# Folding a gate into the output projection's weights and moving the modulation's vectors beside the merge

## The chip, the cores and the metric

The kernel runs on one core of one Trainium2 chip. The metric is the device time in microseconds (us) of one execution; less is better. Matrix products run on TensorE (PE), elementwise work on VectorE (DVE), ScalarE (ACT) and GpSimd (POOL). All transfers of this kernel are issued from the queue of SyncE (SP).

## What is computed

One layer of a streaming encoder: 1024 positions, width 1024, all in float32. Cut to what matters here:

```python
mod = (c_act @ w_ada[l] + b_ada[l])[:, None, :]
shift_t, scale_t, gate_t, shift_f, scale_f, gate_f = jnp.split(mod, 6, axis=-1)

h = x * (1.0 + scale_t) + shift_t
proj = h @ w_in[l]
...
o_a = gated_deltanet(...)          # branch A, 8 heads
o_b = chunk_band_attention(...)    # branch B, 16 heads
gate_a, gate_b = jnp.split(jax.nn.sigmoid(gates + b_gate[l]), N_BRANCHES, axis=-1)
merged = gate_a * (o_a @ w_branch_a[l]) + gate_b * (o_b @ w_branch_b[l])
mix = merged @ w_o[l]
x = layernorm(DEEPNORM_ALPHA * x + gate_t * mix, ln1_g[l], ln1_b[l])

h = x * (1.0 + scale_f) + shift_f
u = causal_dwconv(h @ w_up[l], conv_ffn[l]) + b_conv_ffn[l]
...
x = layernorm(DEEPNORM_ALPHA * x + gate_f * ffn, ln2_g[l], ln2_b[l])
```

`mod` has six vectors of 1024. The first two are needed at the very start. The last four, gate_t, shift_f, scale_f and gate_f, are needed from the output projection on; their weights are 1024 x 4096 values (16 MB).

## The kernel before

The stages follow one another: the input h; branch A's eight heads (some 60 to 860 us of the span); branch B's attention, 16 heads (to about 1343); the merge (to 1456); the output projection with the first layer norm (to 1550); the up projection; the down projection and the last norm. Products are made in three passes: each float32 operand is split into a high and a low part (`split`: a cast, on ACT unless another engine is named, then a subtraction), and high x high, high x low and low x high are summed. A block of weights (128 columns) is loaded into `raw`, a tile with three buffers that are given out in turn, in the order of the program, and split into `wh` and `wl`, also three buffers each (`wblock`, `load_split`). The subtraction of a `wblock` is POOL's.

A planner orders each engine's instructions: among those that its timeline takes for ready, the one that comes first in the program. Each engine, and each DMA queue, then works in the order given.

**The modulation** (`mod_rows`, lines 804 to 827) runs within the loop over branch A's heads, two calls for each head h, 16 in all. A call handles half of the rows of `w_ada` for a block of 512 columns: two loads of 512 KB into `raw`, four DVE instructions that multiply by a column of silu(c) and add into an accumulator (the buffers `gt`, which the merge gates' tiles use too). Behind every second call a product by a matrix of ones sums over the partitions (a full float32 product, two passes on PE), `b_ada` is added to one row, and the row is stored to the DRAM scratch `mod_d`.

**The merge** (lines 1030 to 1067) has 16 blocks: for branch `br` 0 and 1, and j from 0 to 7, a weight block of `w_branch`, 48 products of 128 x 128 by 512, and for each half the gate from scratch (`gates_d`). Branch 0's result stays in the tiles `ma`. Branch 1's is added to it by POOL and split into `mh` and `ml`, which lie where branch A's output was. Behind blocks 5, 6 and 7 of branch 0 the attention's output is loaded and split (`ob`, eight tiles, written to `OB`'s slots); behind branch 1's blocks the eight blocks of `w_o` are loaded and split into `wo`, which take the slots of `ma` and of `ob` as these come free. `OB[i]` and `MA[i]` are lists of slots. Slot B4 holds the attention's group `X` (the buffers `phx`, `plx`), and after it the group `M`, with the ring `macc`.

**The output projection** (`mix`, lines 1102 to 1110) makes 48 products for each of the eight row tiles. Then DVE multiplies the result in PSUM by `gtb` (gate_t / 2, broadcast over the partitions; the half is that of the gates' tanh form), adds ALPHA x, takes statistics, and `norm` applies them on ACT. PE transposes the normed tile, ACT scales and shifts it to the next stage's h (`g1f`, `b1f`), and it is split into `mh` and `ml`. For the scaling, shift_f and scale_f were read back from `mod_d` into rows (`mrow`) and transposed on PE. Of the last row tiles, sums and differences (T2, T3, T4) are built for the up projection, whose products are arranged in a Strassen-like scheme of seven.

Of the kernel before, what the change touches and what calls it, by code (L numbers as in the profile page):

```python
# [73 lines left out]
def _at(group, step_, n, first=0):  # L74
# [30 lines left out]
    "gb": _at("GB", 512, 2), "macc": _at("M", 0, 1),   # L105
    "st": _at("ST", 12, 2), "mv": _at("ST", 4, 4, 36), "gtb": (_E1[0],), "g1b": (_E1[1],),
# [48 lines left out]
def hybrid_layer(  # L155
# [646 lines left out]
    macc = [None]  # L802

    def mod_rows(i):

        cb = i // 2
        if i % 2 == 0:
            macc[0] = ring("gt", [P, 512])
        acc = macc[0]
        for k0 in range(4 * (i % 2), 4 * (i % 2) + 4, 2):  # L810
            rv = W.tile([P, 2, 512], F32, tag="raw", bufs=RB, name=nm("raw"))
            SP.dma_start(rv, w_ada2[k0 * P:(k0 + 2) * P,
                                    2 * D + 512 * cb:2 * D + 512 * cb + 512].rearrange(
                                        "(k p) n -> p k n", p=P))
            for k in (k0, k0 + 1):
                if k == 0:
                    DVE.tensor_scalar(acc, rv[:, 0, :], csil[:, 0:1], None, ALU.mult)
                else:
                    DVE.scalar_tensor_tensor(acc, rv[:, k - k0, :], csil[:, k:k + 1], acc,
                                             ALU.mult, ALU.add)  # L820
        if i % 2 == 1:
            pr_ = mtile(nm("pmod"), "i")
            PE.matmul(pr_, ones, acc, start=True, stop=True)
            row = ring("gt", [P, 512])[0:1, :]
            SP.dma_start(row, b_ada[:, 2 * D + 512 * cb:2 * D + 512 * cb + 512])
            DVE.tensor_tensor(row, row, pr_[0:1, :], ALU.add)
            SP.dma_start(mod_d[:, 512 * cb:512 * cb + 512], row)

# [12 lines left out]
    for h in range(HA):  # L841
        ORD = "sigKq"
        for o in ORD:
            if o == "s":
                with tc.high_priority(offset=PF):
                    stage_solve(h, cs[h])
            elif o == "i":
                with tc.high_priority(offset=PI):
                    stage_inverse(h, cs[h])
            elif o == "K" and h + 1 < HA:  # L850
                with tc.issue_after(last.ins) if last else nullcontext():
                    cs.append(stage_k(h + 1))
            elif o == "g":
                some_gates(GA[h])
            elif o == "q" and h + 1 < HA:
                stage_q(h + 1, cs[h + 1])
        some_gates(GB[h])
        for i in (2 * h, 2 * h + 1):
            mod_rows(i)
        if h + 1 < HA:  # L860
            stage_vz(h + 1, cs[h + 1])
        with tc.high_priority(offset=PC):
            stage_chain(h, cs[h])
        with tc.high_priority(offset=PT):
            stage_out(h, cs[h])
        last = cs[h]["last"]
# [162 lines left out]

    wo = []  # L1030
    for br in range(2):
# [4 lines left out]
        for j in range(NK):  # L1036
            w = wblock(kview(wbr[br], j * P, P), NK)
            for n in range(2):
# [11 lines left out]
                else:  # L1050
# [17 lines left out]


    def bcast(key, src):  # L1070
        t_ = ring(key, [P, D])
        SP.dma_start(t_, src.partition_broadcast(P).rearrange("p o n -> p (o n)"))
        return t_
# [22 lines left out]
    gtb = bcast("gtb", mod_d[:, 0:D])  # L1096
    g1b = bcast("g1b", ln1_g)
    b1b = bcast("b1b", ln1_b)
    DVE.tensor_scalar(gtb, gtb, 0.5, None, ALU.mult)
# [13 lines left out]
    mrow = ring("macc", [P, P])[0:16, :]  # L1113
    SP.dma_start(mrow, mod_d[:, D:3 * D].rearrange("o (r p) -> (o r) p", p=P))
    pmr = pbank("pmr", "t")
    PE.transpose(pmr[:, 0:16], mrow, ident[0:16, 0:16])
    aff = cst.tile([P, 24], F32, tag="aff", name="aff")
    g1f, b1f, s1 = aff[:, 0:8], aff[:, 8:16], aff[:, 16:24]
    g1c, b1c = vt[:, VO["ln1g"]:VO["ln1g"] + 8], vt[:, VO["ln1b"]:VO["ln1b"] + 8]
    DVE.tensor_scalar(s1, pmr[:, 8:16], 1.0, None, ALU.add)  # L1120
    DVE.tensor_tensor(g1f, s1, g1c, ALU.mult)
    DVE.tensor_tensor(b1f, s1, b1c, ALU.mult)
    DVE.tensor_tensor(b1f, pmr[:, 0:8], b1f, ALU.add)
# [3 lines left out]
    for t in range(NT):  # L1127
# [5 lines left out]
        for n in range(2):  # L1133
            N = slice(512 * n, 512 * n + 512)
            DVE.tensor_tensor(m_[:, N], ps[n], gtb[:, N], ALU.mult)
            if t >= MS:
                DVE.scalar_tensor_tensor(r[:, N], r[:, N], ALPHA, m_[:, N], ALU.mult, ALU.add)
        if t < MS:
            DVE.scalar_tensor_tensor(r, r, ALPHA, m_, ALU.mult, ALU.add)
# [26 lines left out]
        if t < NT - 1:  # L1166
            split(mh[:, t], ml[:, t], h32, DVE, DVE)
# [408 lines left out]
```

## Time and profile before

| | |
|---|---|
| median of three runs | 2240.79 us (2235.49 to 2244.45) |
| profiled execution, its own time | 2240.64 us |
| its span, first to last instruction | 2238.9 us |
| mean granted TensorE clock | 0.982 |
| busy share of the span | PE 95%, DVE 71%, ACT 46%, POOL 28% |
| DMA | 220.48 MB, mean 98 GB/s |

The profile is one execution on the chip. Times in it are us from the start of the span. A row of a group gives line, engine, operation, the tile written and those read, shape and count; then busy us, the mean ns of one, and the idle time just before them with what ended most of it. In a timeline, a row is start and duration, and the idle time before it stands in brackets; several instructions of one kind in a row are merged (x2). Rows with SPq are DMA issues. A matmul's duration holds its pipeline, so the distance between two is shorter than one lasts. Line numbers are those of the kernel before.

### The profile page before, as it was taken

Reading aid. Unit: us, or ns where it says so; the run is one execution under the profiler, and the core shown is the slowest. Engines: PE = TensorE matmul, PEld = TensorE weight load, DVE = VectorE, ACT = ScalarE, POOL = GpSimd, SP = SyncE. Lnnn points to the kernel's source line nnn. Section 1 sums busy time; section 2 is a strip of 40 time slices with the busy share of each in tenths; the row PEclk is TensorE's granted clock in tenths of the full one; section 3 lists DMA queues with packets and bytes.
Section 4 is the critical chain, followed back from the end, with each engine's and each line's share of the span. In section 5 each row is a group of like instructions: output and inputs, shape, how many; then the busy total and the mean of one; then the engine's idle time right before and its main releaser. Section 6 shows DMA issues by size and latency. Waiting matters only on the chain.

```text
span 2238.9 us, 31612 instructions
## 1 busy us (share of the span) xinstructions
PE 2129.2 (95%) x11469; PEld 1782.0 (80%) x11469; DVE 1585.5 (71%) x3233; ACT 1025.3 (46%) x2193; POOL 617.0 (28%) x558
## 2 busy tenths in 40 slices
PE   6998999999999999999999999999899999999987
PEld 5687787777878787798989788887688888888875
DVE  8568575765758754567775643458898888889998
ACT  4645243433424334567765642224554444445532
POOL 4323232322323322233432423334110000000064
PEclk9999999999999999999999999999999999999998
DMA  9232333423242412211211523332222222253213
GB/s 284 84 111 73 90 101 105 120 65 117 74 123 80 125 33 98 68 54 47 80 46 59 167 85 128 108 132 94 66 94 85 85 85 85 85 207 110 106 48 131
DMA packets 227263, 220.48 MB, mean 98 GB/s; under 512 B 27354, under 2 KB 184467, under 8 KB 227107
## 3 DMA queue, kind: packets, MB, share of 16 engines
q1 hardware_dynamic: 227027, 218.44, 30.8%
q8 instruction: 90, 1.47, 0.3%
q14 instruction: 66, 0.54, 0.1%
q10 hardware_dynamic: 80, 0.03, 0.0%
HBM read 177.48 MB, written 47.23 MB: 100 GB/s over the span
## 4 chain that ended last, share of the span: by engine, by line
PE 45%; DVE 5%; issue 1%; ACT 1%; POOL 1%; DMA 0%; DVEq 0%; SPq 0%; ACTq 0%; POOLq 0%
PE pup L1282 18%; PE pbr L1043 8%; PE pdn L1460 7%; PE pwo L1107 3%; PE pqk L885 2%; PE pv L900 2%; PE po L975 2%; PE pp L960 1%; PE ps L934 1%; PE pdn L1506 1%; DVE dop L181 0%; DVE hh L1526 0%; DVE hl L181 0%; DMA raw<-in_w_branch_a_dram 0%; DVE G L1163 0%
## 5 line engine op out<-in xcount | busy, mean ns | idle before, releaser
L181 POOL TENSOR_TENSOR wl<-raw,wh 128x1024 fp32r<-128x1024 f32 x88 | 211.4, 2405 | 327.5 <-ACT wh L178 297.9
L1282 PE MATMUL pup<-hh,wop 128*128 128x512 f32 x704 | 229.4, 397 | 5.8 <-ACT SB L1295 3.9
L1282 PE MATMUL pup<-t,wop 128*128 128x512 f32 x792 | 189.9, 393 | 3.9 <-DVE t L181 2.5
L1282 PEld LDWEIGHTS pup<-t,wop 128*128 128x128 f32 x792 | 148.8, 188 | 37.7 <-DVE t L181 2.8
L1282 PEld LDWEIGHTS pup<-hh,wop 128*128 128x128 f32 x704 | 135.0, 192 | 35.4 <-ACT SB L1295 4.3
L178 ACT CAST wh<-raw 128x1024 fp32r<-128x1024 f32 x88 | 92.4, 1050 | 140.1 <-DMA raw<-in_w_in_dram 57.2
L285 PE MATMUL pqkv<-hh,wh 128*128 128x512 f32 x352 | 143.0, 407 | 0.0
L1323 POOL TENSOR_TENSOR cc<-cc,G 128x512 f32<-128x512 f32 x22 | 36.8, 1670 | 378.5 <-DVE G L1305 329.2
L1282 PE MATMUL pup<-hl,wop 128*128 128x512 f32 x352 | 139.9, 398 | 0.9 <-DVE hl L181 0.9
L285 PE MATMUL pqkv<-hl,wh 128*128 128x512 f32 x352 | 140.7, 400 | 0.0
L285 PE MATMUL pqkv<-hh,wl 128*128 128x512 f32 x352 | 139.6, 398 | 0.0
L664 DVE TENSOR_TENSOR FT<-FT,G 128x16 f32<-128x16 f32 (+30 forms) x248 | 120.9, 488 | 19.5 <-POOL G L609 12.2
L178 ACT CAST wop<-wr 128x512 fp32r<-128x512 f32 x110 | 67.1, 621 | 119.7 <-DVE wr L1268 66.5
L945 POOL TENSOR_SCALAR G<-G,FT 128x640 f32<-128x640 f32 (+4 forms) x103 | 69.9, 680 | 183.0 <-DVE FT L944 162.0
L181 DVE TENSOR_TENSOR wop<-wr,wop 128x512 fp32r<-128x512 f32 x110 | 79.5, 731 | 26.2 <-ACT wop L178 25.8
L285 PE MATMUL pgt<-hh,wl 128*128 128x512 f32 x240 | 95.2, 397 | 0.8 <-POOL wl L181 0.8
L285 PE MATMUL pgt<-hh,wh 128*128 128x512 f32 x240 | 95.5, 398 | 0.2 <-DVE tmp L531 0.2
L285 PE MATMUL pgt<-hl,wh 128*128 128x512 f32 x240 | 94.8, 395 | 0.0
L964 DVE TENSOR_TENSOR pl<-pp,ph 128x512 fp32r<-128x512 f32 (+2 forms) x116 | 72.5, 635 | 17.4 <-ACT ph L963 16.6
L1460 PE MATMUL pdn<-hl 128*128 128x512 f32 x324 | 78.0, 394 | 6.1 <-DVE hh L1474 6.1
L1342 DVE SCALAR_TENSOR_TENSOR G<-cc,vt,G 128x1023 f32<-128x1023 f32 (+1 forms) x58 | 75.0, 1297 | 8.1 <-ACT G L1339 8.1
L942 ACT ACTIVATE G<-G,FT 128x640 f32<-128x640 f32 (+4 forms) x103 | 71.6, 695 | 18.9 <-DVE FT L937 16.9
(446 smaller groups left out, 6160.1 us busy)
## 6 DMA issues: line engine op xcount, KB each, us to landing
raw<-in_w_in_dram SPq DMA_DIRECT2D x72, 512.0 KB
wr<-in_w_up_dram SPq DMA_DIRECT2D x44, 512.0 KB
raw<-in_w_ada_dram SPq DMA_DIRECT2D x32, 512.0 KB
dr<-g_d SPq DMA_DIRECT2D x18, 512.0 KB
dr<-in_w_down_dram SPq DMA_DIRECT2D x18, 512.0 KB
wa<-in_w_ada_dram SPq DMA_DIRECT2D x32, 256.0 KB
gates_d<-GT SPq DMA_DIRECT2D x32, 256.0 KB
g_d<-G SPq DMA_DIRECT2D x15, 512.0 KB
```

Source lines behind the costliest of these rows:

```text
L178: ACT.copy(h, src)
L181: return le.tensor_tensor(l, src, f(h), ALU.subtract).ins
L285: PE.matmul(ps, a[:, k, :], r[k][:, 512 * n:512 * n + 512], start=(k == 0 and a is wh and r is rh), stop=(k == NK - 1 and a is wl))
L664: DVE.tensor_tensor(pr[:, :, 0:i + 1], ft[:, :, 0:i + 1], fa[:, i:i + 1, 0:i + 1].to_broadcast([P, 8, i + 1]), ALU.mult)
L942: ACT.activation(sb[:, 0:n], sb[:, 0:n], AF.Exp, bias=mx[:, nb - 1:nb], scale=-1.0, accum_out=mx[:, 2:3])
L945: POOL.tensor_scalar(sb[:, 0:n], sb[:, 0:n], mx[:, 3:4], 0.0, ALU.mult, ALU.add)
L964: DVE.tensor_tensor(pl[:, B, :], pp, f(ph[:, B, :]), ALU.subtract)
L1043: PE.matmul(ps, a[:, k, :], r[k][:, N], start=(k == 0 and a is w[0] and r is rh), stop=(k == NK - 1 and a is w[1]))
L1107: PE.matmul(ps[n], a[:, t, k, :], wo[k][b][:, 512 * n:512 * n + 512], start=(k == 0 and a is mh and b == 0), stop=(k == NK - 1 and a is ml))
L1282: PE.matmul(ps, a[:, u, k, :], b[v][k], start=(new and k == 0 and u == 0 and v == 0), stop=(k == 3 and u == 1), skip_group_check=not new)
L1342: DVE.scalar_tensor_tensor(y[:, d:], cc[:, :S - d], col("conv_f", tap * 44 + ti), y[:, d:], ALU.mult, ALU.add)
L1460: PE.matmul(sets[s_][i], a[:, u, i * P:i * P + P], b[:, v, :], start=(new and j == 0 and u == 0 and v == 0), stop=(j == nq - 1 and u == 1) ...
```

## The change

- The modulation's last four vectors are computed in the merge. `mod_half` replaces `mod_rows`; its 16 calls stand behind branch 0's blocks 5 to 7 and branch 1's blocks 0 to 6 (`MODS`). The accumulators are two buffers in group `M`.
- For shift_f and scale_f the sum over the partitions is taken in the other form: each 128 columns of the accumulator are PE's weights, and the moving operand is one column of ones. The result is a column of 128 values, so nothing is stored and transposed: it goes into `aff` with `b_ada` added.
- `gtb` is loaded behind branch 1's block 0, into `ma`'s first slot. Each block of `w_o` is multiplied by it on DVE ahead of its split. The blocks of `w_o` come one merge block later than before, and use other slots of the two lists.
- At the output projection the multiplication by `gtb` is gone: one DVE instruction for each half adds ALPHA x to the product in PSUM.
- The first cast of seven of the eight tiles' split into `mh` is ACT's instead of DVE's.

```diff
-    "gb": _at("GB", 512, 2), "macc": _at("M", 0, 1),
-    "st": ..., "gtb": (_E1[0],), "g1b": (_E1[1],),
+    "gb": _at("GB", 512, 2), "macc": _at("M", 512, 2),
+    "st": ..., "gtb": (MA[0],), "g1b": (_E1[1],),
...
-    def mod_rows(i):
...
-        for i in (2 * h, 2 * h + 1):
-            mod_rows(i)
...
+    def mod_half(i):
+        cb = i // 2
+        if i % 2 == 0:
+            macc[0] = ring("macc", [P, 512])
+        acc = macc[0]
+        for k0 in range(4 * (i % 2), 4 * (i % 2) + 4, 2):
+            rv = W.tile([P, 2, 512], F32, tag="raw", bufs=RB, name=nm("raw"))
+            SP.dma_start(rv, w_ada2[k0 * P:(k0 + 2) * P,
+                                    2 * D + 512 * cb:2 * D + 512 * cb + 512].rearrange(
+                                        "(k p) n -> p k n", p=P))
+            for k in (k0, k0 + 1):
+                if k == 0:
+                    DVE.tensor_scalar(acc, rv[:, 0, :], csil[:, 0:1], None, ALU.mult)
+                else:
+                    DVE.scalar_tensor_tensor(acc, rv[:, k - k0, :], csil[:, k:k + 1], acc,
+                                             ALU.mult, ALU.add)
+        if i % 2 == 0:
+            return
+        pr_ = pbank(nm("pmod"), "mod")
+        if 2 <= cb < 6:
+            for q in range(4):
+                PE.matmul(pr_[:, q:q + 1], acc[:, q * P:q * P + P], ones[:, 0:1], start=True, stop=True)
+            o, v = 8 + 4 * (cb - 2), VO["b_ada"] + 16 + 4 * cb
+            DVE.tensor_tensor(aff[:, o:o + 4], pr_[:, 0:4], vt[:, v:v + 4], ALU.add)
+        else:
+            PE.matmul(pr_, ones, acc, start=True, stop=True)
+            row = acc[0:1, :]
+            SP.dma_start(row, b_ada[:, 2 * D + 512 * cb:2 * D + 512 * cb + 512])
+            DVE.tensor_tensor(row, row, pr_[0:1, :], ALU.add)
+            SP.dma_start(mod_d[:, 512 * cb:512 * cb + 512], row)
+
+    MODS = {(0, 5): (0, 1), (0, 6): (2, 3), (0, 7): (4,), (1, 0): (5, 6), (1, 1): (7,), (1, 2): (8, 9), (1, 3): (10,),
+            (1, 4): (11, 12), (1, 5): (13,), (1, 6): (14, 15)}
...
+            for i in MODS.get((br, j), ()):
+                mod_half(i)
             if br == 0:
                 for k in {5: (0, 1), 6: (2, 3, 4), 7: (5, 6, 7)}.get(j, ()):
                     load_split(obh[k], obl[k], ob_d[k], ACT, DVE)
-            if br == 1 and (j % 2 == 1 or j == NK - 1):
-                for k in ([j // 2] if j < NK - 1 else range(3, NK)):
-                    at_ = MA[2 * k:2 * k + 2] if k < 4 else OB[2 * k - 8:2 * k - 6]
-                    a, b = (place(o, [P, D], F32R, "wo") for o in at_)
-                    load_split(a, b, w_o2[k * P:k * P + P, :], ACT, DVE)
+            if br == 1 and j == 0:
+                gtb = bcast("gtb", mod_d[:, 0:D])
+                DVE.tensor_scalar(gtb, gtb, 0.5, None, ALU.mult)
+            if br == 1 and j and (j % 2 == 0 or j == NK - 1):
+                for k in ([j // 2 - 1] if j < NK - 1 else range(3, NK)):
+                    a, b = (place(o, [P, D], F32R, "wo") for o in (*MA[1:], *OB[:9])[2 * k:2 * k + 2])
+                    raw = W.tile([P, D], F32, tag="raw", bufs=RB, name=nm("raw"))
+                    SP.dma_start(raw, w_o2[k * P:k * P + P, :])
+                    DVE.tensor_tensor(raw, raw, gtb, ALU.mult)
+                    split(a, b, raw, ACT, DVE)
                     wo.append((a, b))
...
-    mrow = ring("macc", [P, P])[0:16, :]
-    SP.dma_start(mrow, mod_d[:, D:3 * D].rearrange("o (r p) -> (o r) p", p=P))
-    pmr = pbank("pmr", "t")
-    PE.transpose(pmr[:, 0:16], mrow, ident[0:16, 0:16])
...
-            DVE.tensor_tensor(m_[:, N], ps[n], gtb[:, N], ALU.mult)
-            if t >= MS:
-                DVE.scalar_tensor_tensor(r[:, N], r[:, N], ALPHA, m_[:, N], ALU.mult, ALU.add)
-        if t < MS:
-            DVE.scalar_tensor_tensor(r, r, ALPHA, m_, ALU.mult, ALU.add)
+            DVE.scalar_tensor_tensor(r[:, N], r[:, N], ALPHA, ps[n], ALU.mult, ALU.add)
...
-            split(mh[:, t], ml[:, t], h32, DVE, DVE)
+            split(mh[:, t], ml[:, t], h32, ACT, DVE)
```

More of the change, by code (lines that the diff above doesn't have):

```diff
@@ L800, in gate_block @@
             SP.dma_start(gates_d[j][:, N], gt_)
-    macc = [None]
-    def mod_rows(i):
[L806 to L827, printed above, removed]
     gate_block(0)
@@ L1028, in hybrid_layer, with bcast @@
         load_split(oahk[k], oalk[k], oa_d[k], ACT, POOL if k in OL else DVE)
+    def bcast(key, src):
+        t_ = ring(key, [P, D])
+        SP.dma_start(t_, src.partition_broadcast(P).rearrange("p o n -> p (o n)"))
+        return t_
+    aff = cst.tile([P, 24], F32, tag="aff", name="aff")
+    macc = [None]
+    def mod_half(i):
[30 more added lines that the diff above has]
+            (1, 4): (11, 12), (1, 5): (13,), (1, 6): (14, 15)}
     wo = []
```

17 lines of the change are left out of this document (5 added, 12 removed).

## The prediction

> **What bounds the kernel now.** I read the page first (shares, chain), then the stretches of the span, then the groups and waits of the stages that the change touches.
>
> ```profile
> span 2238.9 us, 31612 instructions
> PE 2129.2 (95%) x11469; PEld 1782.0 (80%) x11469; DVE 1585.5 (71%) x3233; ACT 1025.3 (46%) x2193; POOL 617.0 (28%) x558
> PE 45%; DVE 5%; issue 1%; ACT 1%; POOL 1%; DMA 0%; DVEq 0%; SPq 0%; ACTq 0%; POOLq 0%
> ```
>
> PE is the bound: 95% busy, and 45 of the 53% of the span that the chain can be followed back through. A step matters here if it adds or removes PE work, or opens or closes a gap on PE. So the next view is where PE has gaps: the heads (60 to 860 us), the merge (1343 to 1456), the output projection (to 1550), its tail.
>
> ```profile
> core 0: us, PE busy (x) PEld busy (x) DVE busy (x) ACT busy (x) POOL busy (x), PEclk, DMA share, GB/s
> 60.00:860.00 800.00, 763.85 (x4570) 630.07 (x4569) 525.55 (x1311) 329.96 (x881) 236.59 (x230) 0.99 0.32 94
> 1343.00:1456.00 113.00, 113.00 (x498) 93.30 (x498) 44.07 (x45) 27.93 (x34) 38.28 (x23) 1.00 0.36 118
> 1456.00:1550.00 94.00, 94.00 (x434) 77.12 (x434) 65.52 (x93) 31.08 (x63) 37.15 (x21) 1.00 0.38 127
> 1550.00:1600.00 50.00, 35.88 (x128) 27.03 (x128) 44.44 (x67) 24.02 (x48) 11.22 (x5) 0.83 0.12 42
> ```
>
> PE lacks 36.2 us in the heads (800 - 763.85) and 14.1 us behind the output projection (50 - 35.88, where DVE is at 89%); from 1343 to 1550 it has no gap. The change takes work out of the two stretches with gaps and puts it into the full one.
>
> **Part 1: the modulation leaves the heads.**
>
> ```profile
> L819 DVE SCALAR_TENSOR_TENSOR GT<-raw,csil,GT 128x512 f32<-128x512 f32 x56 | 45.5, 813 | 4.7 <-DMA raw<-in_w_ada_dram 3.5
> L817 DVE TENSOR_SCALAR GT<-raw,csil 128x512 f32<-128x512 f32 x8 | 3.9, 484 | 19.6 <-DMA gates_d<-GT 15.6 <-DMA qk_d<-GT 4.0
> L823 PE MATMUL pmod<-GT,ones x16: 591/592/596, 222.1 to 859.4; 128*128 128x512 f32 x16
> 222.09 1.02 PE L823 MATMUL pmod<-GT,ones 128*128 128x512 f32 x2
> PE pxt L688 <- DMA G<-ft_d: 8.6, 9, 2.6
> PE pks L726 <- DVE SA L741: 4.4, 3, 4.1
> ```
>
> PE: one fp32 product by `ones` is two passes, 1.02 us together; the second lasts 0.59, so it starts 0.43 behind the first, and that is what a pass costs. Sixteen passes: -6.9 us of PE work in a stage that PE nearly fills. DVE: 45.5 + 3.9 us of its 525.55 go, and 19.6 us in which it stood in front of L817 until a gate's store had released the `gt` buffer. Of PE's 36.2 us of gaps its largest wait on DVE is 4.4; that on DMA (8.6) doesn't depend on DVE. Between 0 and -36.2 I take -5, near the DVE row, since the burst of eight multiplies is what queues ahead of the chain's small operations. The SP queue loses 32 loads of 512 KB here. Part 1: -11.9 us.
>
> **Part 2: where the 32 loads go.** This decides. `raw` has three buffers, given out by the order of the program. Behind the weights of the sixth block the new order is: four modulation loads (I call them m0 to m3), ob0, ob1, weights w6, m4 to m7, ob2 to ob4, w7, m8, m9, ob5 to ob7, and w8, the first of the second branch. All ten need an accumulator, and these now lie in `M`, in slot B4, where the attention's `X` lay. The trace shows when B4 comes free, because the old `mrow` (loaded at L1114) was placed there. Of the transfer rows, 159.56 with 164.15, 1350.87 with 1354.13, and 1246.57 give the time from an issue to the first use:
>
> ```profile
> SPq L1114 <- PE po L975: 2.4, 1, 2.4
> 1342.12 0.33 SPq L1114 DMA_DIRECT2D B<-mod_d  x1
> 1343.07 113.37 PE pbr L1043 x498
> 159.56 0.38 SPq L812 DMA_DIRECT2D raw<-in_w_ada_dram  x1
> 164.15 1.54 DVE L819 SCALAR_TENSOR_TENSOR GT<-raw,csil,GT 128x512 f32<-128x512 f32 x2 [0.66 <-DMA raw<-in_w_ada_dram]
> 1350.87 1.63 SPq L186 DMA_DIRECT2D raw<-ob_d  x2
> 1354.13 1.05 ACT L178 CAST G<-raw 128x1024 fp32r<-128x1024 f32 x1 [3.50 <-DMA raw<-ob_d]
> 1246.57 6.31 DMA raw<-in_w_branch_a_dram
> L181 DVE TENSOR_TENSOR ob<-raw,ob 128x1024 fp32r<-128x1024 f32 x3 | 3.7, 1224 | 7.3 <-ACT ob L178 4.3 <-DMA ob_d<-ob 3.0
> 767.82 2.39 POOL L181 TENSOR_TENSOR wl<-raw,wh 128x1024 fp32r<-128x1024 f32 x1 [9.99 <-ACT wh L178]
> ```
>
> So m0, m1 and m2 fill all three buffers and sit there until 1342.1, when the attention's last product lets go. Before the change the ob splits and w6 passed through `raw` in that time. PE works at 113.37 / 498 = 0.228 us per product, 10.9 per block of 48; of the 498, 480 are blocks 7 to 16, so PE finishes the sixth block 18 x 0.228 = 4.1 us after 1343.1, at 1347.2, and then needs w6.
>
> A load takes 4.59 us (issue 159.56, use 164.15), at least 3.26 (1350.87 to 1354.13) and at most 6.31. I take 4.6: it is the moved load itself, and a stretch with about two loads in flight lies between the other rows. Use: m 1.6 us of DVE, ob 1.05 (ACT) + 1.22 (DVE), w 1.05 (ACT) + 2.39 (POOL). By buffer:
> - first: m0 done 1343.7, m3 1349.9, w6 ready 1358.0;
> - second: m1 1345.3, ob0 1352.2, m4 1358.4;
> - third: m2 1346.9, ob1 1353.8, m5 (behind m4) 1360.0, ob2 1366.9, w7 1375.0, ob5 1381.9, w8 1389.9.
>
> PE waits for w6 from 1347.2 to 1358.0, and again for w7 and w8. The second branch starts at 1389.9, where it started at 1456.4 - 8 x 10.9 = 1369.0: **+20.9 us**. The four fp32 passes of the gate's two vectors (1.7 us) lie inside these gaps. With 3.3 us per load the six turns of the third buffer are 7.8 us shorter (+13.1), with 6.3 us 10.2 longer (+31.1).
>
> In the second branch 32 loads share three buffers: 10.7 turns of some 6.6 us are 70 us, less than the seven blocks (76 us), so no further gap. PE gains work there: four fp32 passes (1.7 us), and 16 products of one column, two passes each. Their nearest row:
>
> ```profile
> 57.77 0.61 PE L398 MATMUL pmods<-ones,G 128*128 128x1 f32 x4 [0.98 <-DVE G L366]
> 58.23 0.49 PE L285 MATMUL pfirst<-hl,wh 128*128 128x512 f32 x1
> ```
>
> Four passes in 58.23 - 57.77 = 0.46 us, so 32 take 3.7 us. The transposition of `mrow` (-0.2) goes. Part 2: +20.9 + 1.7 + 3.7 - 0.2 = +26.1 us.
>
> The SP queue issues in order, so a load that waits for its buffer also holds the gates' loads behind it. Three PSUM banks, half a block of 5.5 us each, stand between a late gate and PE: I cost it at nothing, and at one turn, 6.6 us, where that cover is gone.
>
> DVE gains 64 x 0.8 = 51 us and eight products by the gate at 1.22, where 44.07 of 113 us were busy: room enough by these rows. Five of the eight come behind the last block: I cost them at nothing, since two row tiles of products stand on PE ahead of the last `wo`; without that cover 6.1 us.
>
> Whether DVE has that room depends on POOL.
>
> ```profile
> 767.83 2.93 DVE L819 SCALAR_TENSOR_TENSOR GT<-raw,csil,GT 128x512 f32<-128x512 f32 x1
> L181 DVE TENSOR_TENSOR hl<-FT,hh 128x512 fp32r<-128x512 f32 x15 | 14.9, 996 | 22.8 <-ACT hh L178 22.8
> L1051 DVE SCALAR_TENSOR_TENSOR FT<-FT,pbr 128x512 f32<-128x512 f32 x15 | 10.3, 687 | 22.6 <-PE pbr L1043 20.5 <-DMA FT<-gates_d 2.0
> ```
>
> A multiply that began 0.01 us behind POOL's split at 767.82 lasted 2.93 instead of 0.75 us. In the merge the subtraction of the same size, from two tensors in SBUF, averages 996 ns, while the one that reads PSUM (L1051) has its 687. So each moved multiply would cost 0.3 us more: 64 x 0.3 = 19 us of DVE, and some 3 to 5 us on the third buffer's path. This is a rival below and not in my sum, as L819 averages 813 in the heads, +0.06.
>
> The Trainium skill, page "SBUF — State Buffer", section "SBUF: two separate sides", states that DVE and GpSimd share a port pair which the first to start holds for its whole instruction, against a DVE instruction with two SBUF inputs while GpSimd reads SBUF. The row of 2.93 us agrees; by the rule alone the time would be the rival's 2251, not 2247.
>
> **Part 3: the gate leaves the output projection.**
>
> ```profile
> L1135 DVE TENSOR_TENSOR G<-pwo,gtb 128x512 f32<-128x512 f32 x16 | 10.4, 683 | 3.5 <-PE pwo L1107 3.5
> L180 DVE CAST hh<-G 128x1024 fp32r<-128x1024 f32 x7 | 7.6, 1083 | 13.4 <-ACT G L1159 13.3
> 1527.67 2.57 DVE L1139 SCALAR_TENSOR_TENSOR G<-G 128x1024 f32<-128x1024 f32 x1
> 1537.73 2.87 DVE L1137 SCALAR_TENSOR_TENSOR r<-r,G 128x512 f32<-128x512 f32 x1
> 1549.06 2.85 DVE L1137 SCALAR_TENSOR_TENSOR G<-G 128x512 f32<-128x512 f32 x1
> 1535.39 0.68 DVE L180 CAST hh<-G 128x1024 fp32r<-128x1024 f32 x1
> PE pn L1156 <- ACT G L1093: 3.6, 1, 3.6
> ```
>
> Up to 1550 PE covers DVE, so only what shortens DVE's queue ahead of the last row tile counts: there the transpositions wait for that tile's norm (3.6 us), and PE's products for what follows. For the last three row tiles go six multiplies (4 us) and three casts of 0.68 us (2 us); the three stretched additions (2.57, 2.87, 2.85) become PSUM readers of 0.69 us a half, up to 5.7 us less, of which I take half, since POOL's instructions stay and will meet others. ACT takes the casts at 1.05 us, seven in 31.08 of 94 busy us: hidden but for about 1 us of latency. Sum -7.5, which comes off the 14.1 us gap: bounds 0 (PE then waits for DVE's building of T2 to T4 instead) and -14.1. Fewer loads around 1456 (the gate's row, `mrow`) I cost at nothing, since PE covers them.
>
> **Sum:** -11.9 + 26.1 - 7.5 = +6.7 us on the profiled run's 2240.64 (its span is 2238.9, with 1.7 around it; the median is 2240.79): **2247 us**. A difference of 0.5%, 11 us, is about what can be told from no change.
>
> **The rivals.** *Slower: the loads take as long as the loaded row.* The crowded stretch asks for three 0.5 MB loads per 6.6 us, 240 GB/s, plus gates; the 6.31 us stood in a crowded place too. Then +10.2: 2257 us. It decides from 5.4 us a load (4.6 + 4.5/6). *The port,* as above: +4 or so, 2251. *Faster: the wait for `raw` isn't there*, if the attention's last head ends 15 us earlier against the merge's products, with ACT and DVE free of five ob splits: 2247 - 21 = 2226. Against it: the wait on B4 is a row of the trace. *Faster by the heads:* if 24 of the 36.2 us of gaps go, 2247 - 19 = 2228; DVE's largest row holds 4.4 of them. *No effect but moved work:* 2240.
>
> **How the numbers follow.** The forecast, within 0.5% (2238 to 2252), 0.34; slow loads (2257) 0.31; the port (2251, and half of it beyond 2252) 0.10; no effect 0.06; `raw` not waited for 0.10, heads 0.09. Faster 0.19, same 0.45, slower 0.36. The range leaves out the ends: 2227 to 2263.
>
> **What would show it.** Right: PE gaps of some 11, 5 and 4 us between the end of the attention and the second branch, ended by the split of w6, w7, w8; the first multiply of the modulation right behind the attention's last product; PE work in the heads down by 7 us; the gap behind the output projection near 7 us. Wrong: no gap on PE in the merge, multiplies that begin before the attention ends, or heads shorter by 20 us or more.

## The result, and the profile after

The median after is 2268.05 us (2267.75 to 2268.34), that of before, run beside it on the same chip, 2239.28 us: a ratio of 1.0119, 95% interval 1.0106 to 1.0132. The medians differ by 28.8 us, the two profiled spans by 27.4; +6.7 was forecast, and 2268 lies outside the range of 2227 to 2263. The profiled execution took 2268.03 us. From the page of the kernel after:

```profile
span 2266.3 us, 31675 instructions
PE 2136.8 (94%) x11492; PEld 1783.4 (79%) x11492; DVE 1573.9 (69%) x3224; ACT 1034.4 (46%) x2202; POOL 616.8 (27%) x558
PE 39%; DVE 8%; DMA 5%; issue 2%; ACT 1%; POOL 0%; SPq 0%; DVEq 0%; ACTq 0%; POOLq 0%
PE pup L1288 18%; PE pdn L1466 6%; PE pwo L1122 3%; PE pbr L1058 3%; DMA raw<-in_w_ada_dram 3%; PE pqk L856 2%; PE pv L871 2%; PE po L946 2%; PE pp L931 1%; PE ps L905 1%; DVE B L1025 1%; DMA raw<-ob_d 1%; DVE hl L181 1%; DMA raw<-in_w_o_dram 1%; DVE dop L181 0%
```

PE's share of the chain fell from 45% to 39%; DMA went from 0% to 5%, and the modulation's loads, on no chain before, now hold 3% of the span. To see where the time goes, I cut the span at three products: the first of branch 0 (`pbr<-hh,wh`), the first of branch 1 (`pbr<-ob,wh`) and the last of the output projection (`pwo<-wo,hl`). A row of a tile's view gives the durations in ns (min/median/max), then the first and the last start. Before:

```profile
L1043 PE MATMUL pbr<-ob,wh x192: 388/390/398, 1368.8 to 1454.5; 128*128 128x512 f32 x192
L1043 PE MATMUL pbr<-hh,wh x128: 387/390/797, 1254.0 to 1368.1; 128*128 128x512 f32 x128
L1107 PE MATMUL pwo<-wo,hl x128: 388/391/481, 1457.2 to 1550.0; 128*128 128x512 f32 x128
```

After:

```profile
L1058 PE MATMUL pbr<-ob,wh x192: 387/389/1415, 1369.4 to 1483.2; 128*128 128x512 f32 x192
L1058 PE MATMUL pbr<-hh,wh x128: 387/389/796, 1233.3 to 1365.8; 128*128 128x512 f32 x128
L1122 PE MATMUL pwo<-wo,hl x128: 389/392/628, 1472.9 to 1583.5; 128*128 128x512 f32 x128
```

| stretch | before | after | difference | forecast |
|---|---|---|---|---|
| A: start to branch 0's first product (heads) | 1254.0 | 1233.3 | -20.7 | -11.9 |
| B: to branch 1's first product | 114.8 | 136.1 | +21.3 | +20.9 |
| C: to the projection's last product | 181.2 | 214.1 | +32.9 | +5.2 |
| D: to the end | 688.9 | 682.8 | -6.1 | -7.5 |
| sum | | | +27.4 | +6.7 |

So two sums came out near the forecast, and two did not: C above all. What PE waited for in B (first line) and in C (total, times, longest):

```profile
PE pbr L1058 <- ACT wh L178: 12.6, 3, 5.4
...
PE pmod L1036 <- DVE B L1025: 8.4, 2, 7.7
PE pwo L1122 <- ACT wo L178: 4.7, 1, 4.7
PE pmod L1032 <- DVE B L1025: 4.4, 2, 2.7
```

In B it is the split of the next weights, three times, as forecast. In C it is mostly the product by `ones`, which waits for its accumulator (12.8 of 17.5 us); PE works in order, so a block of 48 products waits behind it. Waits alone don't fill the stretches. Behind a wait PE ran at a lower granted clock for some 5 us. In these rows the first figures are the window and its length, and the third from the end is PE's granted clock, 1 being full speed:

```profile
1332.00:1337.00 5.00, 4.48 (x10) 3.08 (x11) 2.38 (x4) 0.09 (x1) 2.36 (x1) 0.50 0.59 208
1352.40:1357.00 4.60, 4.14 (x9) 2.85 (x10) 3.10 (x4) 0.04 (x1) 2.37 (x1) 0.50 0.42 126
1373.50:1379.00 5.50, 5.50 (x18) 4.70 (x19) 1.08 (x2) 1.05 (x1) 1.24 (x1) 0.54 0.57 191
1436.00:1441.00 5.00, 5.00 (x17) 3.93 (x16) 3.15 (x3) 1.04 (x1) 2.37 (x1) 0.66 0.76 238
1457.00:1462.00 5.00, 5.00 (x13) 3.33 (x14) 0.60 (x2) 0.00 (x0) 0.00 (x0) 0.65 0.49 161
1497.60:1503.00 5.40, 5.36 (x16) 4.30 (x17) 3.28 (x5) 1.92 (x4) 0.00 (x0) 0.64 0.56 185
```

Length times what the clock lacks is 2.5 + 2.3 us in B and 2.5 + 1.7 + 1.8 + 1.9 in C. With the forecast's 1.7 us of products by `ones` in B and 5.4 in C, B is 12.6 + 4.8 + 1.7 = 19.1 of its 21.3, and C is 17.5 + 7.9 + 5.4 = 30.8 of its 32.9. Why PE waits at all is in the chain (start, duration, what):

```profile
1373.70 4.28 DMA raw<-in_w_ada_dram
1378.08 2.37 DVE B L1023
...
1382.83 5.20 DMA raw<-in_w_ada_dram
1388.12 2.83 DVE B L1025
1392.50 5.38 DMA raw<-in_w_ada_dram
...
1444.31 3.71 DMA raw<-in_w_ada_dram
...
1450.56 4.70 DMA raw<-in_w_ada_dram
```

It goes from a load to a multiplication to the next load, since a buffer of `raw` must be used up before it is loaded again (a turn). From 1373.70 to 1450.56 the chain passes ten loads into `raw`, eight of them the modulation's: nine turns of 8.5 us, where the forecast had 6.6. The issues of the queue say the same. The 32 loads that the second branch puts through `raw` (22 of the modulation, seven of weights, three of w_o) begin and end with these two:

```profile
1362.08 0.38 SPq L1018 DMA_DIRECT2D raw<-in_w_ada_dram  x1
...
1466.34 0.38 SPq L186 DMA_DIRECT2D raw<-in_w_branch_b_dram  x1
```

That is 104 us (the block w8 is issued among them), where the forecast had 70, and where seven blocks of products give 76. The 28 us too many are about what C grew by (32.9) without PE's added products (5.4).

### The profile page after: what moved, and what is told of

Its sections match the earlier page's. It is cut to its first block, busy times and chain, and to the rows that moved or that the text cites. A ratio compares the mean times of both kernels' runs of the same rounds, so it can differ in the third digit from the quotient of the medians.

```text
span 2266.3 us, 31675 instructions
## 1 busy us (share of the span) xinstructions
PE 2136.8 (94%) x11492; PEld 1783.4 (79%) x11492; DVE 1573.9 (69%) x3224; ACT 1034.4 (46%) x2202; POOL 616.8 (27%) x558
## 3 DMA queue, kind: packets, MB, share of 16 engines
q1 hardware_dynamic: 226979, 218.41, 30.2%
## 4 chain that ended last, share of the span: by engine, by line
PE 39%; DVE 8%; DMA 5%; issue 2%; ACT 1%; POOL 0%; SPq 0%; DVEq 0%; ACTq 0%; POOLq 0%
PE pup L1288 18%; PE pdn L1466 6%; PE pwo L1122 3%; PE pbr L1058 3%; DMA raw<-in_w_ada_dram 3%; PE pqk L856 2%; PE pv L871 2%; PE po L946 2%; PE pp L931 1%; PE ps L905 1%; DVE B L1025 1%; DMA raw<-ob_d 1%; DVE hl L181 1%; DMA raw<-in_w_o_dram 1%; DVE dop L181 0%
## 5 line engine op out<-in xcount | busy, mean ns | idle before, releaser
L935 DVE TENSOR_TENSOR pl<-pp,ph 128x512 fp32r<-128x512 f32 (+2 forms) x116 | 72.5, 635 | 19.9 <-ACT ph L934 19.4
L1122 PE MATMUL pwo<-wo,hh 128*128 128x512 f32 x256 | 76.6, 406 | 5.1 <-ACT wo L178 4.7
```

Of the source, the lines that this page charges most:

```text
L935: DVE.tensor_tensor(pl[:, B, :], pp, f(ph[:, B, :]), ALU.subtract)
L1122: PE.matmul(ps[n], a[:, t, k, :], wo[k][b][:, 512 * n:512 * n + 512], start=(k == 0 and a is mh and b == 0), stop=(k == NK - 1 and a is ml))
```

## The experiments

All are medians of 4 to 10 executions against the kernel before, on one chip per group. The letters are the stretches above, read in each trace, as differences to the kernel before in us. A trace is one execution: most lay within 4 us of their kernel's median, e6_pool's 5.8 and e18_shared's 6.7 below it, so a few us between two kernels' stretches are not certain. e8_half, e9_half_dve, e10_half_loads and e15_none leave work out, so their modulation vectors are not the reference's; they only price that work.

| kernel | us | ratio (95%) | A | B | C | D |
|---|---|---|---|---|---|---|
| e1_fold | 2232.6 | 0.9962 (0.9949 to 0.9975) | +1.3 | -1.3 | -0.2 | -8.2 |
| e2_move | 2276.6 | 1.0161 (1.0137 to 1.0185) | -17.9 | +19.6 | +38.0 | -0.2 |
| e3_own | 2244.5 | 1.0019 (1.0007 to 1.0032) | -21.1 | +1.2 | +28.2 | -5.8 |
| e4_early | 2258.4 | 1.0080 (1.0061 to 1.0098) | -20.4 | +9.5 | +34.1 | -6.2 |
| e5_defer | 2243.1 | 1.0009 (0.9999 to 1.0019) | -23.0 | +0.2 | +30.2 | -5.6 |
| e7_defer_shared | 2264.1 | 1.0102 (1.0087 to 1.0117) | -20.1 | +19.9 | +31.2 | -7.5 |
| e6_pool | 2258.3 | 1.0073 (1.0053 to 1.0094) | +18.6 | +0.6 | -0.1 | -7.4 |
| e8_half | 2226.0 | 0.9935 (0.9919 to 0.9952) | -6.1 | -0.4 | -0.2 | -8.2 |
| e9_half_dve | 2239.8 | 0.9997 (0.9985 to 1.0009) | -22.7 | +1.8 | +24.8 | -6.0 |
| e10_half_loads | 2236.1 | 0.9982 (0.9971 to 0.9994) | -23.0 | +1.1 | +20.1 | -5.6 |
| e13_split8 | 2221.5 | 0.9915 (0.9895 to 0.9935) | -27.5 | +2.2 | +13.3 | -7.7 |
| e14_split4 | 2227.0 | 0.9927 (0.9898 to 0.9956) | -11.3 | +2.7 | +3.2 | -6.0 |
| e15_none | 2215.4 | 0.9885 (0.9863 to 0.9907) | -23.2 | 0.0 | -0.4 | -5.4 |
| e16_early | 2219.9 | 0.9902 (0.9890 to 0.9915) | -23.5 | -0.5 | +8.7 | -6.2 |
| e17_dense | 2220.7 | 0.9905 (0.9892 to 0.9917) | -21.4 | +1.5 | +10.1 | -8.1 |
| e18_shared | 2235.1 | 0.9973 (0.9962 to 0.9985) | -24.6 | +6.9 | +11.1 | -5.6 |

In e15_none planning let some products of branch 1 run early, so its B and C are cut at the first product from which they run on (1345.6).

### One part of the change alone

e1_fold, against the kernel after:

```diff
+    def mod_rows(i): ...                    # in the heads, as before
-            for i in MODS.get((br, j), ()):
-                mod_half(i)
+    mrow = ring("macc", [P, P])[0:16, :]    # shift_f, scale_f transposed, as before
```

> The gate folded into w_o's weights as in the change, the modulation left in the heads as before (with its transposed rows). Theory A (three raw buffers, given out in program order, become the chain once the modulation's loads pass through them; the fold itself is cheap): the merge has no gap on PE, the heads keep their 36 us of gaps, the output projection keeps the 13 us that the change's trace gained there: 2239 - 13 = 2226, or 2231 if PE still waits some 5 us for the first wo. Rival B (the fold is part of the damage: the multiplication by the gate stands in the way of the wo splits): 2239 or more, with a gap of 5 us or more on PE ahead of the first products by wo.

Measured 2232.6. The fold costs nothing (B and C as before) and its whole gain is D's 8.2 us. My 13 us was booked wrongly: in the change 40 of the projection's 384 products had been done before 1498, the time that I counted from.

e2_move, against the kernel before: `mod_rows` out, `mod_half` and `MODS` in as in the change; `gtb`, the output projection and w_o's loads as before.

> The modulation moved into the merge as in the change, but the gate stays at the output projection as before, and the wo loads one block earlier as before. Theory A: the two parts add, so the time is the change's plus the 13 us of the output projection: about 2281, with the second branch some 40 us longer than before. Rival B (the fold is part of the damage): the second branch is shorter than in the change by its multiplications and its gtb wait, 2268 or less.

Measured 2276.6: the damage is there without the fold, with D unchanged. C is 5 us larger than in the change, but this trace lay 3.6 us above its median. Rival B falls; theory A's number was too high by the wrongly booked 5 us.

### The buffers

e3_own, against the kernel after (from branch 0's sixth block on, `wh` and `wl` turn over two buffers):

```diff
-            rv = W.tile([P, 2, 512], F32, tag="raw", bufs=RB, name=nm("raw"))
+            rv = place(("W5", "W8")[k0 // 2 % 2], [P, 2, 512], F32, "rmod")
```

> The change, but the modulation's loads get two buffers of their own (the third wh and the third wl, so that weight blocks have two of each); loads, DVE and POOL work stay the same. Theory A: the second branch loses most of its extra 41 us, to 5 to 15 us; the stretch from the sixth block to the second branch stays at +15 to +21, since SP's queue is in order and the third modulation load waits for an accumulator: 2235 to 2245. Rival C (DVE, stretched by POOL, or the bandwidth of the transfers, is what the merge lacks): the second branch stays within 8 us of the change's 128 us: 2260 to 2275.

e4_early, against the kernel after:

```diff
-            macc[0] = ring("macc", [P, 512])
+            macc[0] = place(("SA", "SB")[cb], [P, 512], F32, "macc") if cb < 2 else ring("macc", [P, 512])
```

> The change, but the first two accumulators lie in the slots of ma's seventh and eighth tile (free when the attention's second last head is done) instead of slot B4 (free at the attention's end). Theory A: the first multiplications begin some 10 to 15 us before the attention ends, and the stretch from the sixth block to the second branch shrinks from +21 to 5 to 11 over the 42.2 us of its products' own time; the second branch keeps its +41: 2255 to 2260. Rival C (DVE or bandwidth): the earlier start is lost again behind DVE or the transfers: 2265 to 2270.

e4_early came out as expected: B's +21 is +9.5. In e3_own B's loss is gone altogether. The accumulators still lie in B4, so it is the shared `raw` that carried their wait to the weights. One thing isn't separated here: e3_own also has two load buffers more (five instead of three, at the price of the third `wh` and `wl`), and no run gave the shared ring five. But C lost only 4.7 of its 32.9, where I expected it to lose most. The rows that bound C in e3_own:

```profile
L1065 PE MATMUL pbr<-ob,wh x192: 387/389/1415, 1348.9 to 1461.4; 128*128 128x512 f32 x192
L1129 PE MATMUL pwo<-wo,hl x128: 388/392/478, 1464.1 to 1558.3; 128*128 128x512 f32 x128
```

PE's longest wait in it, again at a product by `ones`:

```profile
PE pmod L1038 <- DVE B L1041: 4.9, 1, 4.9
```

So for C theory A fell as it stood, though 2244.5 lies in its range: that is luck, as B gave some 15 us more than expected, and C less.

### PE's order

e5_defer is e3_own, e7_defer_shared the kernel after, with this edit:

```diff
-        if i % 2 == 0:
-            return
-        pr_ = pbank(nm("pmod"), "mod")
+        if i % 2:
+            held.append((cb, acc))
+    def mod_sum(cb, acc):                   # called behind the next block
+        pr_ = pbank(nm("pmod"), "mod")      # "mod": (7, 3, 4) instead of (7,)
```

> The kernel e3_own (two buffers of their own for the modulation's loads), in which the sum over the partitions on PE is put one block later in the program and has three PSUM banks instead of one. Loads, multiplications and products stay the same. Theory P (PE works in the program's order, so a product by ones that waits for its accumulator, or for the one bank, holds the next block's 48 products): of e3_own's 13 us of gaps between the start of the second branch and the end of the output projection 8 go, and with them products that ran at half speed behind gaps: 2229 to 2237. Rival Q (the work behind those products, DVE's and the SP queue's, is late anyway): the gaps come back as waits for the next weights or gates, 2241 to 2246.

> The change with the same delay of the product by ones (one block later, three banks), the loads still in the shared raw. Theory P: the 12.8 us of PE's waits at those products go, the 21 us ahead of the second branch stay, since they are the raw buffers': 2253 to 2259. Rival Q: the second branch's loss belongs to the raw buffers too, and PE waits for the weights instead: 2264 to 2270.

Theory P fell: against e3_own and the change these runs gain 1.5 and 4 us. In e5_defer no product by `ones` waits any more, and the wait came back later, at w_o, whose splits stand behind the last multiplications on DVE:

```profile
PE pwo L1133 <- ACT wo L178: 8.8, 1, 8.8
PE pbr L1067 <- DVE FT L1075: 5.0, 2, 3.7
PE pbr L1067 <- POOL wl L181: 2.9, 2, 2.0
```

What PE waits for in C is interchangeable: whatever is behind the stream is late.

### The heads

e8_half and e6_pool, against e1_fold:

```diff
-                else:
+                elif k in (3, 5, 7):        # e8_half

-                    DVE.scalar_tensor_tensor(acc, rv[:, k - k0, :], csil[:, k:k + 1], acc, ...)
+                POOL.tensor_scalar(acc if k == 0 else part, part, csil[:, k:k + 1], 0.0, ALU.mult, ALU.add)   # e6_pool
+                if k:
+                    POOL.tensor_tensor(acc, acc, part, ALU.add)
```

> The kernel e1_fold with half of the modulation's 64 multiplications left out (one for each load stays, so the four vectors are not the reference's); loads and PE's products stay. Theory H: half of the 14 us of gaps in the heads go, 2224 to 2227. Rival L (the loads on SP's queue): unchanged, 2231 to 2234.

> The kernel e1_fold (gate folded, modulation in the heads) with the modulation's multiplications on POOL, two instructions for each (a product by the column, a sum) instead of one on DVE. Loads and PE's products stay. Theory H (the 21 us that the change gained in the heads are 7 us of PE work, and 14 us of gaps that came from DVE's 49 us of multiplications standing ahead of the chain's small operations): the merge starts 10 to 14 us earlier than in e1_fold, 2219 to 2223. Rival L (they came from the loads on SP's queue, or POOL's own small operations now wait behind the burst): 2230 or more.

Branch 0's first product in e1_fold:

```profile
L1048 PE MATMUL pbr<-hh,wh x128: 387/389/496, 1255.3 to 1368.1; 128*128 128x512 f32 x128
```

in e8_half:

```profile
L1048 PE MATMUL pbr<-hh,wh x128: 387/389/628, 1247.9 to 1361.6; 128*128 128x512 f32 x128
```

and in e6_pool:

```profile
L1047 PE MATMUL pbr<-hh,wh x128: 387/389/795, 1272.6 to 1387.3; 128*128 128x512 f32 x128
```

Half of DVE's multiplications are worth 7.4 us. If the other half is worth as much (an estimate, and the split runs below show that the price bends), all are worth some 15, and with PE's 6.9 that is A's 21. So e8_half (2226.0) speaks for theory H, and against the loads of rival L, which all stay in it. e6_pool missed H's number: on POOL the same multiplications cost 17 us of A (26 by the medians) instead of saving any. That is L's other half, that POOL's own small operations wait behind them; no run here shows by which path.

### Loads or multiplications

Both against e5_defer:

```diff
-                else:
+                elif k in (3, 5, 7):                                     # e9_half_dve

-            rv = place(OWN[k0 // 2 % 2], [P, 2, 512], F32, "rmod")
-            SP.dma_start(rv, ...)
+            if k0 % 4 == 0:                                              # e10_half_loads
+                rv = place(OWN[i % 2], [P, 2, 512], F32, "rmod")
+                SP.dma_start(rv, ...)
```

> The kernel e5_defer with half of the modulation's 64 multiplications left out (one for each load stays, so the four vectors are not the reference's); loads and PE's products stay. In e5_defer 212 us pass from the start of the second branch to the end of the output projection, against 182 before the change. Theory D (DVE's multiplications, in one queue with the gates' and w_o's work, set that stretch): most of the 24 us beyond PE's added work go, 2219 to 2226. Theory L (the loads' landing, through two buffers, sets it; a turn gets shorter only by the 0.8 us of one multiplication): 2234 to 2243.

> The kernel e5_defer with half of the modulation's loads left out (each load is used by four multiplications instead of two, so the four vectors are not the reference's); DVE's and PE's work stays. Theory D: 2238 to 2244. Theory L: eleven loads fewer in the second branch, and the stretch loses most of its 24 us: 2219 to 2227.

e9_half_dve came in theory L's range; e10_half_loads (2236.1) came in neither, 9 us above L's and 2 below D's. Half of the multiplications took 5.4 us off C, half of the loads 10.1, of e5_defer's 30.2 (3.2 and 7.0 us by the medians). Both count, the loads more, and neither alone is the cause.

### How much of the stream

e13_split8, e14_split4, e16_early, e17_dense and e18_shared are e1_fold with `mod_half` in both places: the first blocks of columns in the heads, the others in the merge as in e5_defer (e18_shared: through `raw`).

```diff
+    HM = {h: (h, h + 1) for h in (0, 2, 4, 6)}                     # heads; e14: twelve half-blocks
+    MM = {(0, 6): (8,), (0, 7): (9,), (1, 0): (10,), ... (1, 5): (15,)}   # e13
+    MM = {(1, 0): (12,), (1, 1): (13,), (1, 2): (14,), (1, 3): (15,)}     # e14
+    MM = {(0, 5): (8,), (0, 6): (9,), ... (1, 4): (15,)}                  # e16, e18
+    MM = {(1, 0): (8, 9), (1, 1): (10, 11), (1, 2): (12, 13), (1, 3): (14, 15)}   # e17
```

(Two runs before these, e11_split8 and e12_split4, 2252.5 and 2249.7 us, put the halves of a block into different heads; a gate's tile took the accumulator in between, so their vectors are not the reference's. Branch 0's first product came at 1262.0 in both, later than in e1_fold, and nothing is drawn from them.)

> Gate folded; gate_t and shift_f are computed in the heads (each block of columns whole, in every second head), scale_f and gate_f in the merge, one half-block behind each block from the seventh on, in two buffers of their own and with the product by ones one block later. Theory A (the merge hides a thin stream; it is the density of 1.5 half-blocks a block in e5_defer that costs): half of the heads' 21 us is gained, the merge costs PE's added 3 us: 2232.6 - 10 + 3, 2223 to 2228. Rival M (each half-block costs the merge the same, 24 us for sixteen beyond PE's work): 2234 to 2239.

> As e13_split8, but only gate_f (four of sixteen half-blocks) is computed in the merge, behind the first four blocks of the second branch, ahead of most of the w_o loads. Theory A: a quarter of the heads' 21 us is gained, the merge costs 1 to 2 us of PE: 2227 to 2230. Rival M: 2233 to 2236.

> The change with the modulation's last four vectors left out altogether (they are zero): no loads, no multiplications, no products by ones, neither in the heads nor in the merge; the fold stays. Its distance to the change is the whole price of the modulation in the merge, its distance to e1_fold the whole price in the heads. If the heads' 21 us and the merge's 54 us add as read from the traces: 2232.6 - 21, 2210 to 2214. If the heads' gain is partly a shift (given back in the attention or the merge): 2216 or more.

e15_none came between its two numbers. It gives the whole price at either place: 2268.0 - 2215.4 = 53 us in the merge, 2232.6 - 2215.4 = 17 in the heads; 4 to 6 when half of it is in each and the merge's half has its own buffers (e13_split8, e16_early, e17_dense), 12 in e14_split4 and 20 in e18_shared. e13_split8 came 1.5 us below theory A's range, but by luck: A gained 29 us over e1_fold where 10 were expected, and B and C lost 17 where 3 were. Half of the stream is nearly free in the heads: branch 0's first product in e15_none (no stream):

```profile
L1063 PE MATMUL pbr<-hh,wh x128: 387/389/796, 1230.8 to 1344.9; 128*128 128x512 f32 x128
```

in e13_split8 (eight half-blocks in the heads):

```profile
L1069 PE MATMUL pbr<-hh,wh x128: 387/389/796, 1226.5 to 1342.6; 128*128 128x512 f32 x128
```

and in e14_split4 (twelve):

```profile
L1069 PE MATMUL pbr<-hh,wh x128: 387/389/792, 1242.7 to 1359.0; 128*128 128x512 f32 x128
```

With all sixteen (e1_fold) it is 1255.3, so the price lies in the second half. Amount and spacing change together, though: the eight stand in every other head, the twelve in six of the eight. In the merge C grows by 3.2 us with four half-blocks, 8.7 to 13.3 with eight, 28.2 and 30.2 with sixteen: a bend too, if a weaker one.

> As e13_split8 (half of the modulation in the heads, half in the merge, one half-block behind each block, own buffers), but the stream in the merge begins one block earlier, behind the sixth block, and so ends behind the second branch's fifth block. In e13_split8 PE waited 5.3 us for a block of w_o, split behind the last multiplications. Theory W (the stream's end runs into the loading and splitting of w_o): that gap goes, 2214 to 2218. Rival: the gap comes back elsewhere, 2220 to 2224.

> As e13_split8, but the eight half-blocks of the merge stand behind the second branch's first four blocks, two behind each. Theory A (density costs): behind each of these blocks four loads need two turns of the two buffers, some 12 us, more than a block's 10.9, and DVE has 6.5 us of multiplications beside the block's own work: some 4 to 8 us slower than e16_early, 2220 to 2226. Rival (only the amount and the meeting with w_o count): the same as e16_early within 2 us, since this stream ends even earlier.

> As e16_early, but the modulation's loads in the merge go through the shared raw (three buffers for all, three weight blocks), as in the change. Theory A (the first loads fill raw and wait for the accumulator in slot B4, and with the shared ring each weight block waits for the multiplications ahead of it): PE gets gaps before the seventh to ninth block again, smaller than the change's 13 us since two loads, not four, stand ahead of each weight block: 5 to 12 us slower than e16_early. Rival (only density counts, the ring doesn't matter for a thin stream): the same within 2 us.

In e16_early PE's wait for w_o shrank from 5.3 to 3.3 us and did not go, so theory W fell; 2219.9 against 2221.5 is within the intervals. e17_dense is the same as e16_early, as its rival said. But the planner began its multiplications at 1321 (its fence below), some 40 us ahead of their place in the program, so on the chip the stream wasn't dense, and this run doesn't tell density from amount. e18_shared costs 15 us over e16_early (9 by the two traces): three shared buffers instead of five, of which two are the stream's own, have a price even for half the stream. The accumulations in e16_early, by their tile:

```profile
L823 DVE SCALAR_TENSOR_TENSOR B<-rmod,csil,B x28: 743/752/2976, 1316.8 to 1384.7; 128x512 f32<-128x512 f32 x28
```

in e17_dense:

```profile
L823 DVE SCALAR_TENSOR_TENSOR B<-rmod,csil,B x28: 739/752/2953, 1321.6 to 1401.0; 128x512 f32<-128x512 f32 x28
```

in e18_shared:

```profile
L822 DVE SCALAR_TENSOR_TENSOR B<-raw,csil,B x28: 737/752/2856, 1313.5 to 1409.4; 128x512 f32<-128x512 f32 x28
```

PE's largest wait in e18_shared from 1314 to 1544 is at the weights again (in e16_early the 3.3 us at w_o is the largest):

```profile
PE pbr L1066 <- ACT wh L178: 6.3, 2, 3.2
```

The same 16 loads and 32 multiplications take 68 us in two own buffers and 96 in three shared ones. The whole stream in e5_defer:

```profile
L1027 DVE SCALAR_TENSOR_TENSOR B<-rmod,csil,B x56: 735/752/2935, 1318.0 to 1448.4; 128x512 f32<-128x512 f32 x56
```

and in the change:

```profile
L1025 DVE SCALAR_TENSOR_TENSOR B<-raw,csil,B x56: 732/752/2830, 1319.1 to 1469.2; 128x512 f32<-128x512 f32 x56
L1023 DVE TENSOR_SCALAR B<-raw,csil x8: 474/488/2357, 1318.5 to 1448.0; 128x512 f32<-128x512 f32 x8
```

It begins at some 1318, when B4 is free, and takes 130 us in its own buffers, 150 in the shared ones. Without it (e15_none) the branch's last product is done at 1432.8, 115 us after 1318. The whole stream doesn't fit ahead of the branch's end, where w_o's splits stand behind it; half of it does.

e16_early is the version to keep: 2219.9 us, 0.9902 (0.9890 to 0.9915) of before, not told apart from e13_split8 and e17_dense.

## Why the prediction was wrong, step by step

- **Part 1, the heads: -11.9, measured -20.7.** The term that was mis-sized is the -5 for gaps: I took the largest row that names DVE (4.4). e8_half puts the multiplications at some 15 us by the estimate above. The stretch A as a window (length, then PE's busy time and instructions, PEld, DVE, ACT, POOL, PE's clock), before:

```profile
0.00:1254.00 1254.00, 1180.01 (x7240) 1001.27 (x7240) 834.09 (x2168) 607.19 (x1529) 401.61 (x425) 0.98 0.32 95
```

and after:

```profile
0.00:1233.30 1233.30, 1167.56 (x7224) 991.66 (x7224) 784.94 (x2096) 610.05 (x1531) 398.89 (x425) 0.99 0.28 83
```

PE's idle time fell from 74.0 to 65.7 us, 8.3 instead of 5. Its busy time fell by 12.4: 6.9 for the sixteen passes, as forecast, and 5.5 that the other products took less, with the clock at 0.99 instead of 0.98. The same shows in e8_half, where products took 5.1 of the 7.4 us less (PE busy 1178.2 us up to branch 0's first product, against 1183.3 in e1_fold). That the clock falls behind a gap was in no term of the sum. As to the gaps, a row names only what came last before PE: waits that name ACT shrank too. Two of PE's waits in the heads before:

```profile
PE pk L573 <- ACT y L542: 2.8, 3, 1.5
PE pu L736 <- ACT SA L733: 2.3, 5, 0.8
```

and the same after:

```profile
PE pu L736 <- ACT SA L733: 0.7, 2, 0.4
...
PE pk L573 <- ACT y L542: 0.5, 1, 0.5
```

- **Part 2, the wait for B4: +20.9, measured +21.3.** The step holds: the first multiplication starts at 1318.5, right behind the attention's last product that reads from B4,

```profile
1318.23 0.28 PE L946 MATMUL po<-B,v 128*64 128x256 f32 x1
```

the first weights wait, and e4_early (half of it gone) and e3_own (all gone) confirm slot and ring. That the sum came so close was luck: the gaps are 4.5, 5.4 and 2.8 us instead of 11, 5 and 4, and some 5 us of PE at half clock, which I had not counted, made up most of the rest.
- **Part 2, the second branch: the step that failed.** "10.7 turns of some 6.6 us are 70 us, less than the seven blocks (76 us), so no further gap." The load was right (3.7 to 5.4 us for `w_ada` in the chain, I took 4.6). A turn measured 8.5 us along the chain, since between a load and the next stand stretched multiplications (2.4 to 2.8 us in the chain rows) and DVE's other work; 10.7 of these are 91 us, and the 32 loads in fact took 104. And a margin of 6 us in 76 was no ground for "no gap". Here too the half clock behind the gaps (7.9 us in C) was in no term. e5_defer, e9_half_dve and e10_half_loads show that no single user of the turn is to blame.
- **The three covers.** "DVE has room" was true by the busy share and false in order: the multiplications stand ahead of gates and w_o (in e5_defer PE waited 5.0 us for a gate's work on DVE and 8.8 for w_o). In the change w_o's five late blocks, costed at nothing or 6.1 without cover, had a wait of 4.7, and no wait of PE names a gate.
- **Part 3: -7.5, measured -6.1 (and -8.2 in e1_fold).** The sum was right, the way to it only in part. The 90 us behind the projection's last product, before:

```profile
1550.00:1640.00 90.00, 75.88 (x304) 59.98 (x304) 80.44 (x111) 45.25 (x77) 16.06 (x8) 0.91 0.20 64
```

and after:

```profile
1583.50:1673.50 90.00, 78.62 (x328) 62.68 (x328) 79.50 (x112) 47.50 (x80) 12.83 (x6) 0.94 0.22 71
```

The gap shrank by 2.7 us, from 14.1 to 11.4, and not to near 7; the clock of 0.94 instead of 0.91 is worth as much again.
- **The rivals.** Slow loads did not come. The port: in the merge the accumulation's mean is 902 ns against 813 in the heads, so 0.1 us each instead of the rival's 0.3; single ones took up to 2.8 us. The Trainium skill, page "SBUF — State Buffer", section "SBUF: two separate sides", has a DVE instruction with two SBUF inputs and a GpSimd instruction that reads SBUF exclude each other on a shared pair of ports for the whole instruction. The maxima of 2.8 to 3.0 us agree, though no run isolates the lock. Heads 24 us better: near in size (20.7), and "heads shorter by 20 us or more", a sign of being wrong that I had named, came; but it did not decide.

**Open.** How C's 30 us in own buffers divide: PE's added products are some 5.4, the rest is waits and half-clock stretches behind loads and multiplications together. Whether five shared buffers would do as well as two of the stream's own, and whether density or amount makes the price bend. Why PE still waits 3.3 us for w_o in e16_early, and not in e1_fold, was not tried.

## What to carry to other kernels

Work that is moved into a stage without gaps must fit there from the moment its buffers come free to the moment at which the work behind it in the same queues is needed, in turns measured with everything else that stands in the same ring and queue; a busy share says nothing of that. A gap on PE cost more than its length here, since the products behind it ran at a lower clock. The price bends: half of the work hid in each of two places, and all of it cost 17 us in one and 53 in the other, so try a split before a move. A shared ring hands one late user's wait to all others; two more buffers, the stream's own, took 24 us off this change (2268.0 to 2244.5).

## What the runs showed of the hardware

PE's granted clock was 0.50 for some 5 us behind waits of 4.5 and 5.4 us, products starting 0.43 us apart instead of 0.23; these two gaps cost about half as much again as their length. The Trainium skill, page "TensorE: Matmul & The Clock Gate", section "Part 1: The HAM clock gate (the "warmup" mystery)", has the array at half clock after an idle window of about 3.4 us and back after one of work. The two rows at 0.50 agree. The row of 1436 to 1441, at 0.66, does not by itself: it followed a wait of 1.7 us and eight one-column passes (1.0 us), and no run here separates the two.
